# Clipped difference moved to ScalarE, a second load of x by rows, a gathered bias, and a grouped norm that runs behind, in a two-layer hybrid encoder

## The chip, the cores and the metric

One core of a Trainium2 chip runs the whole step. The metric is the device time of one execution in microseconds. Engines are named as in the profile: PE (TensorE), PEld (its weight loads), DVE (VectorE), ACT (ScalarE), POOL (GpSimd), SP (SyncE, which issues every DMA of this kernel).

## The reference

Two layers work on 1024 prompt tokens and 64 sample tokens, width 1024. Each layer normalises x, projects it to 5204 columns, runs three branches on them (RG-LRU, sparse attention with an indexer and top-k, Mamba-2 SSD), and adds the projected mix to x. Cut to what the change touches:

```python
h = x * rsqrt(mean(x * x, -1) + eps) * norm_w                  # first norm of a layer
# SSD, in chunks; cum is the cumulated dt * a of a head
decay = exp(where(tril, cum[l] - cum[s], -inf))
y = (decay * (C @ B.T) * dt) @ xs + exp(cum) * (C @ state) + D * xs
y = y * silu(z)
y_c = rmsnorm(y.reshape(..., 2, 512)) * ssd_norm               # grouped norm
# attention over the selected keys
logits = q @ k.T / 8 + rel_bias[bucket(pos_k - pos_q)]
```

## The kernel before

Tokens stand in nine tiles of 128 (the ninth has 64) and three chunks CH of 384, 384 and 320 columns. Activations lie with features on the partitions. A projection keeps fp32 precision with three matmuls a block: high and low parts of the weights (`whi`, `wlo`, made on ACT at L212 and on DVE or POOL at L213) times high and low parts of the activations (`sth`, `stl`); lines L235 to L237 are these matmuls.

The first layer's start: `load_x` issues x transposed in eight 128-row pieces for each chunk (L260), and the first norm's sums are made by `first_sums`: a Square of each piece on ACT (L268), additions on DVE (L270), then `token_sums`, three matmuls against ones (L290). `rsqrt` is twelve small DVE operations, and `spread` lays its result out over the columns with one matmul (L281). Then come `hf`, its high and low parts, and the first two projections, of the index keys and index queries.

`spread_bias` runs once, at the end of the first layer's index stage: it multiplies a bucket table of 32x384 with rel_bias (L162), copies the result into a buffer `g2` of the pool that projection outputs also use (L164), and writes it 128 times over to DRAM as `biasd` (L165). `near_bias` reads from it, with a stride of 383, each row's own window of 256 positions (L994), and adds a large number to one block (L996). It is called for each of the two key-value groups of a layer; its tile `nb` has one buffer.

Between the index stage and attention, the top-k bisection (`junk` on DVE at L596, `junka` on ACT at L602), the convolutions (`u`, `th`, `raw`), the gates, the queries and the SSD tiles run interleaved. The order in which steps are written out is the table PLAN: `s0` and `s1` advance the SSD generator of group 0 or 1 by one step. After each projection `pace` advances the top-k by one bit, at a lower priority. Within this, a scheduler orders the instructions of each engine by priority and by its own model of when things are due; the order is then fixed, and each engine runs it in sequence.

`ssd_inputs` prepares a tile: it loads the cumulated sums of eight heads to all partitions (`cumB`, L730, two buffers), transposes, scales, and forms the decay in three steps: for each head, subtract the row's own value and clip at zero (L760, DVE, eight instructions a tile), Exp (L763, ACT), times `cbm` (L764, DVE). `ssd` then does a tile's matmuls and adds, and multiplies with the gate into `yC` (L822). Squares and their sums go to `sqS` on ACT and POOL (L824 to L826). After every third tile the grouped norm follows at once: `token_sums`, `rsqrt`, `spread`, and four DVE products (L837) with four writes to DRAM. `yC` and `sqS` have one buffer each.

Of the kernel before, what the change touches and what calls it, by code (L numbers as in the profile page):

```python
# [10 lines left out]
F32 = mybir.dt.float32  # L11
# [49 lines left out]
def bucket_table():  # L61

    t = np.zeros((32, 384), np.float32)
    for m in range(384):
        rel = m - 255
        n = abs(rel)
        b = max(i for i in range(16) if BUCKET_FROM[i] <= n) + (16 if rel > 0 else 0)
        t[b, m] -= 1.0
        t[15, m] += 1.0
    return t  # L70
# [18 lines left out]
def body(ctx, tc, I, O):  # L89
# [39 lines left out]
    def s2_bank():  # L129
        return bank("s2", 2)  # L130
# [21 lines left out]


    biasd = drp.tile([8, 128, 384], F32, name="biasd")

    def spread_bias(p):
        tab = p.tile([32, 384], F32, name="tab")
        SP.dma_start(tab, I["bucket_table"])
        rb = p.tile([32, 8], F32, name="rb")
        SP.dma_start(rb, I["rel_bias"])  # L160
        bp = s2_bank()
        PE.matmul(bp[:8, :384], rb, tab, start=True, stop=True)  # L162
        bv = lay.tile([128, 384], F32, name="g2", bufs=G2)[:8]
        S.activation(bv, bp[:8, :384], AF.Copy)  # L164
        SP.dma_start(biasd, bv[:, None, :].to_broadcast([8, 128, 384]))  # L165
# [89 lines left out]

    def load_x(ci):
        a, b = CH[ci]
        for d in range(8):
            X[d, ci] = xpool.tile([128, b - a], F32, name=f"X{d}_{ci}")
            SP.dma_start(X[d, ci], I["x_t"][128 * d:128 * d + 128, a:b])  # L260

    def first_sums(ci):

        a, b = CH[ci]
        acc = xpool.tile([128, 384], F32, name="xacc", bufs=2)[:, :b - a]
        for d in range(8):
            sq = xpool.tile([128, 384], F32, name="xsq", bufs=4)[:, :b - a]
            S.activation(sq if d else acc, X[d, ci], AF.Square)  # L268
            if d:
                V.tensor_tensor(acc, acc, sq, op=OP.add)  # L270
        return token_sums(acc, ci)
# [13 lines left out]
    def token_sums(sqs, ci):  # L285

        ps = s2_bank()
        for t in range(3):
            n = rows_of(3 * ci + t)
            PE.matmul(ps[:n, t:t + 1], sqs[:, t * 128:t * 128 + n], ones[:, 0:1], start=True, stop=True)  # L290
        ss = small.tile([128, 3], F32, name="ssg")
        if ci == 2:
            V.memset(ss, 1.0)
            V.tensor_copy(ss[:, :2], ps[:, :2])
            V.tensor_copy(ss[:TS, 2:3], ps[:TS, 2:3])
        else:
            V.tensor_copy(ss, ps[:, :3])
        return ss

    for l in range(DEPTH):  # L300
# [31 lines left out]
        with ExitStack() as st:  # L332
# [11 lines left out]
            if l == 0:  # L344
                load_x(2)
                SP.dma_start(pk[1], I["par"][1])


            for ci, (a, b) in enumerate(CH):
                ss = token_sums(sqs[ci], ci) if l else first_sums(ci)  # L350
# [121 lines left out]
        with ExitStack() as st:  # L472
# [100 lines left out]
            if l == 0:  # L573
                spread_bias(p)
# [142 lines left out]
        def ssd_inputs(g, tt):  # L717
# [40 lines left out]

            for h in range(8):
                V.tensor_scalar(cumB[:n, h, :n], cumB[:n, h, :n], ctk[:n, tt, 8 * g + h:8 * g + h + 1], 0.0,  # L760
                                op0=OP.subtract, op1=OP.min)
            cB = cumB[:n, :, :n]
            S.activation(cB, cB, AF.Exp)  # L763
            V.tensor_tensor(cB, cB, cbm[:n, None, :n].to_broadcast([n, 8, n]), op=OP.mult)  # L764
            return xsc, C_, eB, bt, xdt, xde, cB

        def ssd(g):
# [4 lines left out]
            ready = ssd_inputs(g, 0)  # L772
            for k, tt in enumerate(order):
# [8 lines left out]
                if k % 3 == 0:  # L782
                    yC = p.tile([128, 4, 384], F32, name="yC", bufs=1)
                    sqs = p.tile([128, 384], F32, name="sqS", bufs=1)
# [41 lines left out]
                G.tensor_tensor(sqs[:, cc:cc + n], sq[:, 0, :n], sq[:, 1, :n], op=OP.add)  # L826
                yield
                if k % 3 < 2:
                    continue

                w = b0 - a0
                ss = token_sums(sqs, ci)
                r = rsqrt(ss, 3, 1.0 / 512, "g")
                rp = s2_bank()
                spread(r, 3 * ci, rp)
                for i in range(4):
                    V.scalar_tensor_tensor(yC[:, i, :w], yC[:, i, :w], par[:, 104 + 4 * g + i:105 + 4 * g + i], rp[:, :w],  # L837
                                           op0=OP.mult, op1=OP.mult)
                    SP.dma_start(ycd[4 * g + i][:, a0:b0], yC[:, i, :w])
                yield  # L840
# [150 lines left out]
        def near_bias(g):  # L991

            nb = kp.tile([128, 4, 256], F32, name="nb")
            SP.dma_start(nb, bass.AP(tensor=biasd.tensor, offset=biasd.offset + 4 * g * 128 * 384 + 127,  # L994
                                     ap=[[383, 128], [128 * 384, 4], [1, 256]]))
            V.tensor_scalar(nb[0:64, :, 192:256], nb[0:64, :, 192:256], BIG, None, op0=OP.add)  # L996
            return nb
# [193 lines left out]
def packed(x):  # L1191
# [3 lines left out]
    a = {"rel_bias": f("rel_bias"), "bucket_table": bucket_table()}  # L1195
    a["x_t"] = np.concatenate([f("x_prompt")[0], f("x_sample")[0]]).T
# [55 lines left out]
```

## Time and profile before

| | us |
|---|---|
| median of 3 runs | 2112.63 (2110.53 to 2113.01) |
| the profiled execution's own time | 2118.68 |
| its span in the trace | 2116.9 |
| busy: PE, DVE, ACT, POOL | 1975.6, 1614.3, 1132.9, 654.5 |

How to read the rows below. In a row of busy time by stretch the columns are: the stretch in us from the start; its length; busy us and (x instructions) of PE, PEld, DVE, ACT and POOL, or of one engine where the row is of one line alone; the granted TensorE clock as a share; the DMA engines' busy share; GB/s. A row of the timeline has the start, the duration, engine, line, operation, output<-inputs, sizes and count, and in brackets how long the engine stood before it and what ended that. A row of waits says who waited for whom: us in total, times, longest. In a row of a group the figures behind the bar are busy us and mean ns of one, then idle us before it. Instructions on one engine overlap by some 0.1 us, so eight in a row take less than eight means. A busy PE is not PE at its peak, since matmuls are pipelined.

### The profile page before, as it was taken

The numbers are of one execution on the slowest core, as the hardware profiler recorded it, in microseconds if no ns is written. First come the engines' busy times: TensorE is split into PE (matmuls) and PEld (weight loads), VectorE is DVE, ScalarE is ACT, GpSimd is POOL, SyncE is SP. The second block draws the span as 40 slices with busy tenths as digits, with TensorE's granted clock in tenths as the row PEclk, the third lists the DMA queues.
The fourth block names the chain that finished last, engine by engine and source line by source line (L and its number), as shares of the span: only waits on it lengthen the run. The fifth ranks groups of instructions, "written<-read, shape, count | busy, mean of one in ns | idle before, by whom it ended". The sixth has DMA issues, their size and how long they took to land.

```text
span 2116.9 us, 34794 instructions
## 1 busy us (share of the span) xinstructions
PE 1975.6 (93%) x12076; PEld 1767.8 (84%) x12076; DVE 1614.3 (76%) x4102; ACT 1132.9 (54%) x2244; POOL 654.5 (31%) x561
## 2 busy tenths in 40 slices
PE   5989989888999899999999999988899998999999
PEld 5889988878898788866998999887888897888589
DVE  8668999999886875475287889999998778556723
ACT  5558967622465454445255798664324565444521
POOL 3012243433332332142430222443334225223420
PEclk9999999999999999999999999999999998999999
DMA  4135353353533642332641343534454326334145
GB/s 137 55 64 155 95 143 119 101 172 104 139 90 101 208 143 90 107 100 88 199 143 55 94 116 101 161 106 127 118 153 119 118 104 207 108 91 131 57 132 171
DMA packets 253368, 255.11 MB, mean 121 GB/s; under 512 B 31048, under 2 KB 233192, under 8 KB 253192
## 3 DMA queue, kind: packets, MB, share of 16 engines
q1 hardware_dynamic: 253192, 252.89, 39.9%
q8 instruction: 95, 1.56, 0.3%
q14 instruction: 81, 0.66, 0.1%
HBM read 176.68 MB, written 76.14 MB: 119 GB/s over the span
## 4 chain that ended last, share of the span: by engine, by line
PE 51%; DVE 29%; DMA 9%; issue 5%; ACT 3%; SPq 1%; POOL 1%; DVEq 0%; ACTq 0%; POOLq 0%
PE mm L236 12%; PE mm L237 12%; PE mm L235 11%; PE s L1119 4%; PE tp L1114 3%; PE s L1089 3%; DVE junk L596 3%; DVE u L878 3%; DMA cumB<-cumd 3%; DVE cumB L760 3%; DMA biasd<-g 2%; PE s L534 1%; PE s L904 1%; ACT junka L602 1%; DVE cumB L764 1%
## 5 line engine op out<-in xcount | busy, mean ns | idle before, releaser
L213 POOL TENSOR_TENSOR wlo<-wraw,whi 128x1024 fp32r<-128x1024 f32 x80 | 198.1, 2476 | 390.8 <-ACT whi L212 378.1
L602 ACT ACTIVATE junka<-sc,cand 128x768 bf16<-128x768 f32 x248 | 239.1, 966 | 24.7 <-DVE cand L622 20.6
L212 ACT ACTIVATE whi<-wraw 128x1024 fp32r<-128x1024 f32 x130 | 137.1, 1054 | 148.1 <-PE mm L236 89.3
L1096 ACT ACTIVATE lg<-lg,mx 128x512 f32<-128x512 f32 (+8 forms) x144 | 111.3, 773 | 108.8 <-DVE mx L1092 108.0
L1081 POOL TENSOR_TENSOR nbm<-nb,shared 128x256 f32<-128x256 f32 (+1 forms) x112 | 81.3, 729 | 231.1 <-DVE mx L1092 208.9
L878 DVE SCALAR_TENSOR_TENSOR u<-raw,parh,u 128x384 f32<-128x384 f32 (+1 forms) x198 | 144.7, 736 | 1.9 <-ACT u L872 0.8
L1116 ACT ACTIVATE pT<-tp 128x512 f32<-128x512 f32 (+1 forms) x164 | 90.2, 568 | 101.8 <-PE tp L1114 99.9
L596 DVE TENSOR_SCALAR_CACHE_REDUCE junk<-sc,cand 128x384 bf16<-128x384 f32 (+4 forms) x194 | 140.1, 752 | 0.7
L1089 PE MATMUL s<-kst,qst 128*128 128x512 f32 (+4 forms) x448 | 120.6, 361 | 9.7 <-DVE mx L1092 9.3
L1114 PEld LDWEIGHTS tp<-identr,lg 128*128 128x128 f32 (+2 forms) x656 | 71.8, 140 | 46.9 <-issue 39.7
L1114 PE MATMUL tp<-identr,lg 128*128 128x128 f32 (+2 forms) x656 | 107.3, 278 | 0.7 <-DVE lg L1099 0.7
L1119 PE MATMUL s<-pT,vt 128*64 128x256 f32 (+2 forms) x656 | 103.9, 392 | 1.6 <-ACT pT L1116 1.6
L1099 DVE TENSOR_SCALAR lg<-lg,ri 128x512 f32<-128x512 f32 (+8 forms) x144 | 98.1, 681 | 3.5
L760 DVE TENSOR_SCALAR cumB<-cumB,ctk 128x128 f32<-128x128 f32 (+1 forms) x288 | 83.3, 353 | 22.1 <-DMA cumB<-cumd 19.7
L1164 DVE TENSOR_TENSOR xl<-xl,mm 128x384 f32<-128x384 f32 (+1 forms) x40 | 21.4, 540 | 92.9 <-PE mm L237 84.7
L1089 PEld LDWEIGHTS s<-kst,qst 128*128 128x128 f32 (+1 forms) x448 | 71.5, 187 | 24.0 <-DVE mx L1092 16.4
L1092 DVE CUSTOM_DVE_ANT_0 lg<-s,shared 128x512 f32<-128x512 f32 (+4 forms) x112 | 61.8, 552 | 38.4 <-PE s L1089 32.4
L235 PE MATMUL mm<-sth0a,whi 128*128 128x384 f32 (+1 forms) x228 | 81.5, 360 | 7.8 <-DVE sth0a L974 2.6
L213 DVE TENSOR_TENSOR wlo<-wraw,whi 128x1024 fp32r<-128x1024 f32 x50 | 63.5, 1269 | 26.4 <-ACT whi L212 25.9
L236 PE MATMUL mm<-stl0a,whi 128*128 128x384 f32 (+1 forms) x228 | 79.6, 349 | 2.8 <-POOL stl0a L977 2.5
L798 POOL TENSOR_TENSOR hT<-hT,dec 128x512 f32<-128x512 f32 x28 | 40.7, 1454 | 131.4 <-DMA ycd<-yC 57.7
L236 PE MATMUL mm<-stl7a,whi 128*128 128x384 f32 (+1 forms) x228 | 78.6, 345 | 2.2 <-DVE stl7a L977 2.2
(477 smaller groups left out, 6977.5 us busy)
## 6 DMA issues: line engine op xcount, KB each, us to landing
wraw<-in_w_in_dram SPq DMA_DIRECT2D x82, 512.0 KB, 3.7
wraw<-in_w_out_dram SPq DMA_DIRECT2D x48, 512.0 KB, 4.2
cumB<-cumd SPq DMA_DIRECT2D x32, 512.0 KB, 5.2
xsd<-u SPq DMA_DIRECT2D x48, 192.0 KB, 2.3
gz<-gzd SPq DMA_DIRECT2D x32, 256.0 KB, 3.9
xsc<-xsd SPq DMA_DIRECT2D x32, 256.0 KB, 3.5
eB<-cumd SPq DMA_DIRECT2D x56, 128.0 KB, 3.5
gzd<-g SPq DMA_DIRECT2D x32, 192.0 KB, 1.9
```

What stands on the lines that cost most here:

```text
L212: S.activation(hi, raw, AF.Copy)
L213: eng.tensor_tensor(lo, raw, hi.bitcast(F32), op=OP.subtract)
L235: PE.matmul(ps, hi[:, k, :], xh[ci][:, c0:], start=k == 0, stop=False)
L236: PE.matmul(ps, hi[:, k, :], xl[ci][:, c0:], start=False, stop=False)
L237: PE.matmul(ps, lo[:, k, :], xh[ci][:, c0:], start=False, stop=k == len(xs) - 1)
L596: V.tensor_scalar(junk, sc[j][:n], thr, None, op0=op, op1=OP.add, accum_out=out)
L602: S.activation(junk, sc[j][:n], AF.Sign, scale=-1.0, bias=cand, accum_out=out)
L760: V.tensor_scalar(cumB[:n, h, :n], cumB[:n, h, :n], ctk[:n, tt, 8 * g + h:8 * g + h + 1], 0.0, op0=OP.subtract, op1=OP.min)
L878: V.scalar_tensor_tensor(u, raw[:, j:j + n], w[:, wbase + j * wstride:wbase + j * wstride + 1], u, op0=OP.mult, op1=OP.add)
L1089: PE.matmul(ps[:nq, :b - a], qst[:, h, :nq], kst[:, g, pt, kbase + a:kbase + b], start=pt == 0, stop=pt == 1)
L1114: PE.transpose(ps[:n, i * nq:(i + 1) * nq], lgs[h][:nq, j * 128:j * 128 + n], ident[:nq, :nq])
L1119: PE.matmul(av[64 * b:64 * b + 64, :, :nq], vt[:n, vj, 64 * g:64 * g + 64], pT[:n, 2 * b:2 * b + 2, :nq], start=j == 0, stop=j == nb_ - 1)
```

## The change

Four edits. The bucket table, its matmul and the write of `biasd` go; the host hands over the near bias already gathered by position (an input of 2x128x4x256) and a row of far biases, and `near_bias` loads the first and forms far minus near on DVE, one instruction a head. Each chunk of x is also loaded by rows into `xr` (L246 in the changed kernel), ahead of the transposed pieces, and one Square with an accumulated sum on ACT gives the sums of 128 tokens; `first_sums` goes. The subtraction with its clip becomes a Relu on ACT with a scale of -1 and the row's value as bias, and the Exp takes a scale of -1. The grouped norm is cut into `sums` and `products`, of which one runs at the end of each following SSD tile; after the last tile what is left runs at once. `yC` and `sqS` get the pool's two buffers.

```diff
-    biasd = drp.tile([8, 128, 384], F32, name="biasd")
-    def spread_bias(p):
...
-        PE.matmul(bp[:8, :384], rb, tab, start=True, stop=True)
-        S.activation(bv, bp[:8, :384], AF.Copy)
-        SP.dma_start(biasd, bv[:, None, :].to_broadcast([8, 128, 384]))
...
     def load_x(ci):
         a, b = CH[ci]
+        for t in range(3):
+            n = rows_of(3 * ci + t)
+            xr = xpool.tile([128, DM], F32, name="xr", bufs=6)
+            SP.dma_start(xr[:n], I["x_r"][a + 128 * t:a + 128 * t + n])
+            S.activation(xr[:n], xr[:n], AF.Square, accum_out=ssx[ci][:n, t:t + 1])
         for d in range(8):
...
-                ss = token_sums(sqs[ci], ci) if l else first_sums(ci)
+                ss = token_sums(sqs[ci], ci) if l else ssx[ci]
...
             for h in range(8):
-                V.tensor_scalar(cumB[:n, h, :n], cumB[:n, h, :n], ctk[:n, tt, 8 * g + h:8 * g + h + 1], 0.0,
-                                op0=OP.subtract, op1=OP.min)
-            cB = cumB[:n, :, :n]
-            S.activation(cB, cB, AF.Exp)
+                S.activation(cB[:, h, :], cB[:, h, :], AF.Relu, scale=-1.0, bias=ctk[:n, tt, 8 * g + h:8 * g + h + 1])
+            S.activation(cB, cB, AF.Exp, scale=-1.0)
             V.tensor_tensor(cB, cB, cbm[:n, None, :n].to_broadcast([n, 8, n]), op=OP.mult)
...
+        def grouped_norm(g, ci, yC, sqs):
+            a, b = CH[ci]
+            r = []
+            def sums():
+                r.append(rsqrt(token_sums(sqs, ci), 3, 1.0 / 512, "g"))
+            def products():
+                rp = s2_bank()
+                spread(r[0], 3 * ci, rp)
+                for i in range(4):
+                    V.scalar_tensor_tensor(yC[:, i, :b - a], yC[:, i, :b - a], par[:, 104 + 4 * g + i:105 + 4 * g + i],
+                                           rp[:, :b - a], op0=OP.mult, op1=OP.mult)
+                    SP.dma_start(ycd[4 * g + i][:, a:b], yC[:, i, :b - a])
+                return True
+            return [sums, products]
...
-                    yC = p.tile([128, 4, 384], F32, name="yC", bufs=1)
-                    sqs = p.tile([128, 384], F32, name="sqS", bufs=1)
+                    yC = p.tile([128, 4, 384], F32, name="yC")
+                    sqs = p.tile([128, 384], F32, name="sqS")
...
+                if due and due.pop(0)():
+                    yield
                 yield
...
+                if k % 3 == 2:
+                    due += grouped_norm(g, ci, yC, sqs)
+            for part in due:
+                part()
+            yield
...
-            SP.dma_start(nb, bass.AP(tensor=biasd.tensor, offset=biasd.offset + 4 * g * 128 * 384 + 127,
-                                     ap=[[383, 128], [128 * 384, 4], [1, 256]]))
+            SP.dma_start(nb, I["near_bias"][g])
+            for h in range(4):
+                V.tensor_scalar(nb[:, h, :], nb[:, h, :], far_bias[:, 4 * g + h:4 * g + h + 1], -1.0,
+                                op0=OP.subtract, op1=OP.mult)
```

PE at the very start, before (`xacc` holds summed squares, `dg` the diagonal that `spread` multiplies with ones, `s` and `mm` are PSUM banks):

```order
L290 MATMUL s_263<-ones,xacc 128x1 x3
L290 MATMUL s_407<-ones,xacc 128x1 x3
L281 MATMUL s_269<-dg,ones 128x384
L290 MATMUL s_543<-ones,xacc 128x1 x2
L290 MATMUL s_543<-ones,xacc 64x1
L235 MATMUL mm<-sth0a,whi 128x384
L235 MATMUL mm<-sth0a,whi 128x128
```

The same place in the changed kernel:

```order
L260 MATMUL s_271<-dg,ones 128x384
L215 MATMUL mm<-sth0a,whi 128x384
L216 MATMUL mm<-stl0a,whi 128x384
L217 MATMUL mm<-sth0a,wlo 128x384
L215 MATMUL mm<-sth1a,whi 128x384
```

The sums of all three chunks stood ahead of the first projection matmul; now one spread does, and the two projections of the first chunk (384 and 128 columns wide) no longer alternate.

ACT at the tile of 64 rows and the one behind it in the first layer's SSD group 0, before:

```order
L862 ACTIVATE raw<-mm 128x256
L863 ACTIVATE raw<-mm 128x64
L872 ACTIVATE u<-raw,parh 128x323
L763 ACTIVATE cumB<-cumB 64x8x64
L859 ACTIVATE raw<-mm 128x384
L887 ACTIVATE th<-u 128x384
L746 ACTIVATE bt<-tp 64x128
```

ACT behind the same tile (`bt` 64x128 is its transpose) in the changed kernel:

```order
L724 ACTIVATE bt<-tp 64x128
L863 ACTIVATE u<-raw,parh 128x323
L878 ACTIVATE th<-u 128x384
L739 ACTIVATE cumB<-cumB,ctk 128x128 x8
L850 ACTIVATE raw<-mm 128x384
L580 ACTIVATE junka,cnt<-sc_641,cand 128x768
L580 ACTIVATE junka,cnt<-sc_642,cand 128x896
L740 ACTIVATE cumB<-cumB 128x1024
```

Eight Relus stand in ACT's queue ahead of a copy out of a PSUM bank (`raw`) and of the sign counts; the Exp follows some places behind them.

PE at the end of the first layer's SSD group 1, the last grouped norm, before:

```order
L235 MATMUL mm<-sth2a,whi 128x384
L290 MATMUL s_7468<-ones,sqS 128x1
L290 MATMUL s_7468<-ones,sqS 64x1
L236 MATMUL mm<-stl2a,whi 128x384
L237 MATMUL mm<-sth2a,wlo 128x384
```

The same place in the changed kernel:

```order
L215 MATMUL mm<-sth2a,whi 128x384
L216 MATMUL mm<-stl2a,whi 128x384
L269 MATMUL s_7399<-ones,sqS 128x1
L269 MATMUL s_7399<-ones,sqS 64x1
L217 MATMUL mm<-sth2a,wlo 128x384
```

The last sums stand one matmul further back, within the same projection block.

## Rows read from the trace of the kernel before

**Rows 1.** The page's first part, busy time by engine, and its chain by engine.
```profile
PE 1975.6 (93%) x12076; PEld 1767.8 (84%) x12076; DVE 1614.3 (76%) x4102; ACT 1132.9 (54%) x2244; POOL 654.5 (31%) x561
...
PE 51%; DVE 29%; DMA 9%; issue 5%; ACT 3%; SPq 1%; POOL 1%; DVEq 0%; ACTq 0%; POOLq 0%
```
**Rows 2.** Busy time by stretch, all engines.
```profile
170.00:250.00 80.00, 78.10 (x467) 77.52 (x466) 69.97 (x197) 73.96 (x153) 19.04 (x9) 1.00 0.44 129
250.00:550.00 300.00, 270.34 (x1682) 251.31 (x1680) 288.44 (x698) 153.66 (x309) 112.08 (x83) 0.96 0.44 127
...
1210.00:1290.00 80.00, 80.00 (x482) 79.93 (x481) 70.28 (x199) 75.30 (x157) 19.04 (x9) 1.00 0.46 134
1290.00:1590.00 300.00, 267.65 (x1692) 247.50 (x1691) 289.19 (x702) 153.38 (x307) 114.04 (x83) 0.98 0.43 127
```
**Rows 3.** Busy time by stretch of line L760 alone, on DVE.
```profile
250.00:550.00 300.00, 32.38 (x96) 0.96 0.44 127
550.00:710.00 160.00, 6.50 (x32) 0.99 0.37 114
...
1290.00:1590.00 300.00, 30.91 (x97) 0.98 0.43 127
```
**Rows 4.** Waits over the whole span, around cumB.
```profile
ACT cumB L763 <- DVE cumB L760: 79.1, 26, 5.2
...
DVE cumB L760 <- DMA cumB<-cumd: 19.7, 13, 3.2
```
**Rows 5.** Busy time of the same work in the first and in the second layer.
```profile
108.00:245.00 137.00, 129.38 (x761) 125.09 (x761) 106.38 (x304) 105.03 (x218) 26.00 (x15) 0.98 0.43 110
1159.30:1284.70 125.40, 125.25 (x758) 122.66 (x758) 106.20 (x304) 104.69 (x217) 25.38 (x15) 1.00 0.36 107
```
**Rows 6.** The chain in order of time, and ACT's timeline, at the bias write.
```profile
120.61 33.54 DMA biasd<-g
...
154.23 0.38 ACT L679 ACTIVATE g<-tp 128x256 f32<-128x256 f32 x1 [9.32 <-DMA biasd<-g]
```
**Rows 7.** Busy time by stretch at the start; the last column is GB/s.
```profile
5.00:10.00 5.00, 0.00 (x0) 0.00 (x0) 3.68 (x11) 3.33 (x9) 0.00 (x0) 1.00 0.98 333
10.00:15.00 5.00, 1.44 (x6) 1.35 (x6) 4.40 (x20) 4.20 (x8) 0.00 (x0) 1.00 1.03 375
```
**Rows 8.** Timeline: the first two weight splits; projection matmuls, first, second chunk's, last.
```profile
10.62 1.06 ACT L212 ACTIVATE whi<-wraw 128x1024 fp32r<-128x1024 f32 x1 [1.07 <-DMA wraw<-in_w_in_dram]
...
16.59 1.06 ACT L212 ACTIVATE whi<-wraw 128x1024 fp32r<-128x1024 f32 x1 [1.06 <-DMA wraw<-in_w_in_dram]
...
27.06 0.79 PE L235 MATMUL mm<-sth0a,whi 128*128 128x384 f32 x2 [0.31 <-ACT sth0a L365]
...
38.54 0.39 PE L235 MATMUL mm<-sth0a,whi 128*128 128x384 f32 x1
...
55.95 0.31 PE L237 MATMUL mm<-sth7b,wlo 128*128 128x320 f32 x1
```
**Rows 9.** Near bias: durations of L996 (min/median/max ns), a 128x256 form, POOL's wait.
```profile
L996 DVE TENSOR_SCALAR nb<-nb x4: 277/281/287, 718.6 to 1891.3; 64x256 f32<-64x256 f32 x4
...
L1099 DVE TENSOR_SCALAR lg<-lg,ri 128x256 f32<-128x256 f32 x4 | 1.9, 479 | 0.1
...
POOL nbm L1081 <- DVE nb L996: 12.6, 4, 5.5
```
**Rows 10.** ACT groups by form: two operands per partition, none, and 128 columns.
```profile
L872 ACT ACTIVATE u<-raw,parh 128x384 f32<-128x384 f32 x48 | 33.7, 702 | 11.8 <-DMA xsd<-u 8.0 <-DVE junk L653 3.3
L859 ACT ACTIVATE raw<-mm 128x384 f32<-128x384 f32 x64 | 30.6, 478 | 20.7 <-PE mm L237 20.4
...
L746 ACT ACTIVATE bt<-tp 128x128 f32<-128x128 f32 x32 | 8.6, 270 | 33.0 <-DVE cbm L744 33.0
```
**Rows 11.** PE's wait for the grouped norm's sums, and the later of its places.
```profile
PE s L290 <- POOL sqS L826: 13.5, 2, 7.0
...
1738.31 0.48 PE L290 MATMUL s<-ones,sqS 128*128 128x1 f32 x4
```

More of the change, by code (lines that the diff above doesn't have):

```diff
@@ L58, with buckets @@
 P_DT, P_A, P_D, P_QK, P_ALL = 160, 176, 192, 200, 328
[L61 to L70, printed above, removed]
+def buckets():
+    rel = np.arange(256)[None, :] - np.arange(128)[:, None] - 128
+    return np.searchsorted(BUCKET_FROM, np.abs(rel), side="right") - 1 + 16 * (rel > 0)
 def rows_of(t):
@@ L151, in body @@
         G.memset(kb[:, j:j + 1], float(2 * kk[j] - nks[j] - 1))
-    biasd = drp.tile([8, 128, 384], F32, name="biasd")
-    def spread_bias(p):
[L157 to L161, printed above, removed]
-        PE.matmul(bp[:8, :384], rb, tab, start=True, stop=True)
-        bv = lay.tile([128, 384], F32, name="g2", bufs=G2)[:8]
-        S.activation(bv, bp[:8, :384], AF.Copy)
-        SP.dma_start(biasd, bv[:, None, :].to_broadcast([8, 128, 384]))
     def rsqrt(ss, n, scale, tag, rows=128):
@@ L254, in body @@
     pk = [lay.tile([128, P_ALL], F32, name=f"pk{l}") for l in range(DEPTH)]
+    far_bias = const.tile([128, 8], F32, name="far_bias")
+    ssx = [small.tile([128, 3], F32, name=f"ssx{ci}", bufs=1) for ci in range(3)]
+    V.memset(ssx[2], 1.0)
     def load_x(ci):
         a, b = CH[ci]
+        for t in range(3):
[3 more added lines that the diff above has]
+            S.activation(xr[:n], xr[:n], AF.Square, accum_out=ssx[ci][:n, t:t + 1])
         for d in range(8):
@@ L260, in load_x @@
             SP.dma_start(X[d, ci], I["x_t"][128 * d:128 * d + 128, a:b])
[L262 to L271, printed above, removed]
     def spread(r, t0, dst):
@@ L346, in body @@
                 SP.dma_start(pk[1], I["par"][1])
+                SP.dma_start(far_bias, I["far_bias"])
             for ci, (a, b) in enumerate(CH):
-                ss = token_sums(sqs[ci], ci) if l else first_sums(ci)
+                ss = token_sums(sqs[ci], ci) if l else ssx[ci]
                 rp = s1_bank()
@@ L572, in body @@
             SP.dma_start(cumd, cumt)
-            if l == 0:
-                spread_bias(p)
         steps(zs)
@@ L757, in ssd_inputs @@
                             op=OP.mult)
+            cB = cumB[:n, :, :n]
             for h in range(8):
-                V.tensor_scalar(cumB[:n, h, :n], cumB[:n, h, :n], ctk[:n, tt, 8 * g + h:8 * g + h + 1], 0.0,
-                                op0=OP.subtract, op1=OP.min)
-            cB = cumB[:n, :, :n]
-            S.activation(cB, cB, AF.Exp)
+                S.activation(cB[:, h, :], cB[:, h, :], AF.Relu, scale=-1.0, bias=ctk[:n, tt, 8 * g + h:8 * g + h + 1])
+            S.activation(cB, cB, AF.Exp, scale=-1.0)
             V.tensor_tensor(cB, cB, cbm[:n, None, :n].to_broadcast([n, 8, n]), op=OP.mult)
             return xsc, C_, eB, bt, xdt, xde, cB
+        def grouped_norm(g, ci, yC, sqs):
[12 more added lines that the diff above has]
+            return [sums, products]
         def ssd(g):
@@ L772, in ssd @@
             ready = ssd_inputs(g, 0)
+            due = []
             for k, tt in enumerate(order):
@@ L826, in ssd @@
                 G.tensor_tensor(sqs[:, cc:cc + n], sq[:, 0, :n], sq[:, 1, :n], op=OP.add)
+                if due and due.pop(0)():
+                    yield
                 yield
[L828 to L840, printed above, removed]
+                if k % 3 == 2:
[3 more added lines that the diff above has]
+            yield
         PCH = ((0, 384), (384, 768), (768, PW))
@@ L1194, in packed @@
     tiles = lambda a: a.reshape(DEPTH, -1, 128)
-    a = {"rel_bias": f("rel_bias"), "bucket_table": bucket_table()}
-    a["x_t"] = np.concatenate([f("x_prompt")[0], f("x_sample")[0]]).T
+    b = f("rel_bias")
+    a = {"near_bias": b[buckets()].transpose(2, 0, 1).reshape(2, 4, 128, 256).transpose(0, 2, 1, 3),
+         "far_bias": np.repeat(b[15:16], 128, 0)}
+    a["x_r"] = np.concatenate([f("x_prompt")[0], f("x_sample")[0]])
+    a["x_t"] = a["x_r"].T
     w = f("w_in").reshape(DEPTH, 8, 128, EIN)
```

## The prediction

> **What bounds the kernel now.** I read the engines' busy time and the chain of waits first [rows 1]. TensorE is busy for 1975.6 of 2116.9 us, which looks like the bound, but only 51% of the chain runs through it; VectorE holds 29%. So the bound changes by stage, and the busy time by stretch comes next [rows 2]. Each layer has two kinds of stretch. In 170 to 250 us and 1210 to 1290 us (convolutions and top-k, no SSD tiles) TensorE is busy 78.1 and 80.0 of 80 us. In 250 to 550 us and 1290 to 1590 us (the same loops with the SSD tiles among them) VectorE is busy 288.4 and 289.2 of 300 us, TensorE 270.3 and 267.7, ScalarE 153.7 and 153.4. There VectorE is the bound, at 96%, and TensorE has gaps. The eight subtractions with a clip per tile at L760 are the part of that load which the change takes away: 32.4 and 30.9 us in those two stretches, 6.5 us in 550 to 710 [rows 3]. Their order matters too: VectorE stands 19.7 us there for the transfer of cumB, and ScalarE stands 79.1 us for VectorE before the exponential [rows 4].
>
> Two other places are bound by something else. The stretch from the last index scores to the first SSD tile does the same work in both layers (304 VectorE instructions each), but takes 137.0 us in the first and 125.4 in the second [rows 5]. What only the first has is the write of the bias table: it is on the chain for 33.54 us, and ScalarE stands 9.32 us because the write still reads a buffer that its next output needs [rows 6]. And at the start the transfers run at 333 to 375 GB/s [rows 7], while the first projection matmul comes at 27.06 us [rows 8].
>
> **The change, part by part.**
>
> Bias table gone. The 33.54 us write leaves, with one matmul, one ScalarE copy and three issues on the SP queue. If the first layer then runs as the second does, that is 137.0 - 125.4 = 11.6 us [rows 5]; the least is 0, if the weights behind it on the queue come late anyway. The 9.32 us wait has no other cause [rows 6], so I take -11.
>
> The near bias is loaded ready and corrected: four more VectorE operations of 128x256 at each of four loads. The nearest rows are 281 ns (64 rows, same line) and 479 ns (a 128x256 TENSOR_SCALAR), so 16 x 0.28 to 0.48 = 4.5 to 7.7 us [rows 9]. The load itself stays 512 KB. GpSimd waits for this tile at all four places [rows 9], so nothing covers all of it, but GpSimd is not the bound there: 0 to +8, I take +3.
>
> The start. Sums come from a second load of x by rows: 4.46 MB more on the queue (8 x 512 KB and 256 KB). At 340 GB/s the first 1.57 MB costs 4.6 us, all of it 13. In return 21 VectorE additions, nine matmuls and the order change: before, TensorE does all three chunks' sums ahead of the first projection matmul, now only the first chunk's spread stands there. The first weights' split, at 10.62 us, moves to about 15.2 and ends at 16.3; the first matmul follows at about 17, not 27. It does not all count: the second block's weights are behind x of the second chunk, so their split moves from 16.59 to about 16.6 + 9.2 = 25.8, and its low part ends near 28. From there 2.7 us of narrow matmuls for the first chunk and the second and third chunks, 38.54 to 56.26 before [rows 8], are left: 28 + 2.7 + 17.7 = 48.5 against 56.3. Ends: -11 (the whole earlier start), +13 (every byte late and nothing gained). I take -7.
>
> The clipped difference on ScalarE. Off VectorE go 63.3 us in the two bound stretches. If VectorE stayed the bound, all of it would leave the time; if the queue behind cumB's transfer bound them, none. Between: TensorE gets 482 matmuls through 80 full us [rows 2], so the 1682 and 1692 of the bound stretches need about 279 and 281 us: at most 21 and 19 us can go at that rate. That limit is rough, since the SSD's matmuls are narrower. I take half of VectorE's share, -32, with ends -63 and 0. In 550 to 710 us no engine is alone; 6.5 us goes from VectorE there, I count -1 a layer, so -2.
>
> ScalarE pays for it. An operand per partition costs it (702 - 478) / 2 = 112 ns each, from two 128x384 forms with two and none; a 128x128 copy takes 270 ns, so one Relu is about 380 ns, some 0.3 us in a row [rows 10]: 288 of them 84 us. In the bound stretches it has 146 us of 300 free. In 170 to 250 it has 6 of 80 free, TensorE 2: 16 Relus, 4.8 us a layer, land there ahead of evacuations that TensorE's banks need. 0 to +10 for both layers; I take +6. The wait for cumB moves from VectorE's queue to ScalarE's: behind it stand convolution copies and sign counts, and then VectorE and TensorE. VectorE's 19.7 us [rows 4] bounds that at either engine; it is within the ends above.
>
> The Trainium skill speaks against this move: "ScalarE: Activation LUTs", section "Rules for kernel authors", puts relu, max, min and add on VectorE and not on ScalarE, as VectorE does more elements in a cycle. By that rule the move costs 84 - 63 = 21 us instead of giving 32. The rows for the bound stretches (VectorE 96%, ScalarE 51%) say that here it is the fuller engine that counts.
>
> The grouped norm a tile and two behind. Same instructions. TensorE's wait for its sums is 13.5 us, but in two places alone; one is at 1738.31 us, the end of the second layer's last group, and the other is its like in the first layer [rows 11]. There the new code runs sums and products right after the last tile as before, so this wait stays. The earlier groups show next to none. The four writes of each chunk pass later through SP; who reads them comes at the layer's end. A second buffer of yC frees the next tile: -6 to +6, I take -1.
>
> **Sum.** -11 + 3 - 7 - 32 - 2 + 6 - 1 = -44. The profiled execution took 2118.68 us (span 2116.9), 6 above the median of the runs, 2112.63; the difference applies to either. Predicted: 2112.63 - 44 = 2068.6.
>
> **Rivals.** *VectorE's whole share counts* (-63 rather than -32, ScalarE's +6 gone): -81, 2032 us. For it: 96% busy with next to no waits but cumB's. Against: TensorE's rate gives only 40. *The SSD stage does not shorten*, since the path from cumB's transfer through Relu, exponential and product replaces the one through VectorE: -11 + 3 - 7 = -15, 2098 us. For it: VectorE waits for that transfer now [rows 4], and no buffer is added for it. Against: 300 us hold 96 subtractions [rows 3], twelve tiles, so some 25 us for each. *ScalarE becomes the bound* (slower than before): it takes 84 us of Relus and 20 us of waiting, with PSUM evacuations behind in order. It decides once more than about 15 of these 104 us reach TensorE while the SSD stage gives nothing; with a third, 2112.6 - 15 + 35 = 2133 us. For it: 92 to 94% busy in 170 to 250. Against: the bound stretches have room for it. The Trainium skill's rule above would be this case. *The change does not speed the start*: x twice keeps TensorE waiting as long as before; that is +7 on any case, 2076 on mine.
>
> **How the numbers follow.** My forecast, with the start's rival and a spread of 20 either side, 0.60; whole share 0.14; no shorter stage 0.16; ScalarE bound 0.08; everything cancelling to within 4 us 0.02. The range for 8 in 10 runs from 2034 to 2100: it holds the forecast, most of the no-gain case and half of the whole-share case. About 0.2% (4 us) is what a measurement of this kernel can tell from no change. Faster 0.89, same 0.03, slower 0.08.
>
> **What would show it.** Right: no 9 us ScalarE wait near 145 us and 125 us for the stretch of [rows 5]; first projection matmul near 17 us and the three chunks done near 48; VectorE's share in the SSD stretches under 95% with TensorE's busy share up, each stretch 10 to 21 us shorter; ScalarE busy about 80 us longer. Wrong: ScalarE standing for cumB's transfer as long as the stretch gained, TensorE waiting for bank evacuations in 170 to 250 us, or a second transfer of x that delays the second chunk past 40 us.

## The result, and the profile of the changed kernel

The changed kernel takes 2087.18 us (median of 4 runs, 2084.96 to 2090.63) against 2112.82 us for the kernel before in the same session: a ratio of 0.9881, 95% interval 0.9864 to 0.9898, or -25.6 us. The forecast was -44 with a range of -78 to -12. The time lies in the range and the sign is right, but 18 us of the forecast gain are missing, and they go with one of the four edits, the grouped norm.

The page's busy time by engine and its chain by engine, of the changed kernel, answer to [rows 1]:

```profile
PE 1964.9 (94%) x12056; PEld 1753.2 (84%) x12056; DVE 1542.9 (74%) x3805; ACT 1209.1 (58%) x2525; POOL 652.9 (31%) x561
...
PE 53%; DVE 24%; DMA 9%; ACT 7%; issue 5%; SPq 1%; POOL 1%; DVEq 0%; ACTq 0%; POOLq 0%
```

VectorE has lost 71 us of busy time, and ScalarE has gained 76 (about 80 forecast). Busy time by stretch, with the columns of [rows 2]:

```profile
170.00:250.00 80.00, 78.67 (x477) 77.89 (x476) 71.60 (x194) 76.49 (x162) 17.34 (x7) 1.00 0.32 105
250.00:550.00 300.00, 278.86 (x1760) 255.43 (x1759) 276.36 (x619) 186.79 (x423) 125.03 (x97) 0.98 0.48 136
...
1290.00:1590.00 300.00, 276.45 (x1742) 253.44 (x1742) 275.89 (x609) 185.26 (x414) 122.36 (x96) 0.97 0.46 134
```

In the two stretches that VectorE bound it is now busy 92% of the time instead of 96%, and TensorE is busy 8.5 to 8.8 us more. In 170 to 250 us ScalarE rises to 76.5 of 80 us, and TensorE does not fall.

The start, in the timeline of TensorE: the first projection matmul and the last one of the third chunk, which answer to [rows 8]; and the transfer rate from 5 to 10 us (last column), which answers to [rows 7]:

```profile
15.53 0.69 PE L215 MATMUL mm<-sth0a,whi 128*128 128x384 f32 x1 [2.16 <-ACT sth0a L345]
...
48.65 0.31 PE L217 MATMUL mm<-sth7b,wlo 128*128 128x320 f32 x1
```
```profile
5.00:10.00 5.00, 0.00 (x0) 0.00 (x0) 1.15 (x7) 3.30 (x6) 0.00 (x0) 1.00 1.05 390
```

The first matmul comes at 15.5 us (27.06 before, 17 forecast), and the last matmul of the third chunk starts at 48.65 (55.95 before; the three chunks were forecast to be done near 48). The work of [rows 5], from the last index scores to the first SSD tile, now takes this stretch:

```profile
100.70:228.50 127.80, 126.28 (x769) 122.90 (x768) 105.30 (x285) 107.15 (x231) 25.59 (x16) 1.00 0.36 108
```

It is 127.8 us long instead of 137.0, and the write of the bias table and the wait of 9.32 us behind it [rows 6] are gone with it.

What is new is a group of waits. From the list of waits over the whole span (who waited for whom: us in total, times, longest):

```profile
PE s L260 <- DVE dg L258: 29.8, 8, 11.7
...
PE tp L1013 <- ACT pT L1008: 10.7, 5, 4.8
...
PE mm L215 <- DVE sth0a L965: 9.4, 4, 3.8
...
ACT cumB L739 <- DMA cumB<-cumd: 59.9, 23, 7.6
...
POOL nbm L1074 <- DVE nb L989: 20.5, 4, 8.6
```

TensorE no longer waits for the grouped norm's sums (13.5 us in [rows 11]). It waits for `dg`, the diagonal that `spread` multiplies (9.5 us before), and where attention begins for `pT` (4.4 before; it is the copy of a key tile there) and for `sth0a` (2.6 before). Of the 29.8 us for `dg`, 11.7 are TensorE's first wait of the program, which comes with the new start; the other 18.1 are new waits. The chain in order of time has a piece at the end of the first layer's SSD part that the chain of before did not have among its longest:

```profile
689.24 8.38 DMA lg<-in_cache_att_k_dram
```

`lg` there is the tile into which attention's cached keys are loaded. It belongs to none of the four edits.

### The profile page after: what moved, and what is told of

It is laid out like the page before. It is cut to its first block, busy times and chain, and to the rows that moved or that the text cites. A ratio compares the mean times of both kernels' runs of the same rounds, so it can differ in the third digit from the quotient of the medians.

```text
span 2088.8 us, 34723 instructions
## 1 busy us (share of the span) xinstructions
PE 1964.9 (94%) x12056; PEld 1753.2 (84%) x12056; DVE 1542.9 (74%) x3805; ACT 1209.1 (58%) x2525; POOL 652.9 (31%) x561
## 3 DMA queue, kind: packets, MB, share of 16 engines
q1 hardware_dynamic: 251904, 255.73, 40.2%
## 4 chain that ended last, share of the span: by engine, by line
PE 53%; DVE 24%; DMA 9%; ACT 7%; issue 5%; SPq 1%; POOL 1%; DVEq 0%; ACTq 0%; POOLq 0%
PE mm L216 12%; PE mm L215 12%; PE mm L217 12%; PE s L1112 4%; PE tp L1107 4%; PE s L1082 3%; ACT junka L580 3%; DVE junk L574 3%; DVE u L869 2%; DMA cumB<-cumd 2%; PE s L895 1%; PE s L514 1%; DMA eB<-cumd 1%; ACT cumB L739 1%; DVE cumB L741 1%
## 5 line engine op out<-in xcount | busy, mean ns | idle before, releaser
L869 DVE SCALAR_TENSOR_TENSOR u<-raw,parh,u 128x384 f32<-128x384 f32 (+1 forms) x198 | 138.5, 707 | 7.1 <-ACT u L863 4.5
L739 ACT ACTIVATE cumB<-cumB,ctk 128x128 f32<-128x128 f32 (+1 forms) x288 | 88.6, 384 | 64.5 <-DMA cumB<-cumd 59.9
L1092 DVE TENSOR_SCALAR lg<-lg,ri 128x512 f32<-128x512 f32 (+8 forms) x144 | 90.2, 629 | 2.9
L734 POOL TENSOR_TENSOR xsc<-xsc,pk 128x512 f32<-128x512 f32 (+1 forms) x36 | 46.4, 1288 | 135.5 <-PE tp L728 122.0
L1082 PEld LDWEIGHTS s<-kst,qst 128*128 128x128 f32 (+1 forms) x448 | 70.0, 183 | 20.5 <-DVE mx L1085 11.5
L193 DVE TENSOR_TENSOR wlo<-wraw,whi 128x1024 fp32r<-128x1024 f32 x50 | 62.5, 1250 | 31.6 <-ACT whi L192 31.5
L821 POOL TENSOR_TENSOR sq<-sq 128x256 f32<-128x256 f32 (+1 forms) x36 | 34.9, 969 | 159.6 <-ACT sq L820 159.6
```

Source lines behind the costliest of these rows:

```text
L193: eng.tensor_tensor(lo, raw, hi.bitcast(F32), op=OP.subtract)
L869: V.scalar_tensor_tensor(u, raw[:, j:j + n], w[:, wbase + j * wstride:wbase + j * wstride + 1], u, op0=OP.mult, op1=OP.add)
L1082: PE.matmul(ps[:nq, :b - a], qst[:, h, :nq], kst[:, g, pt, kbase + a:kbase + b], start=pt == 0, stop=pt == 1)
```

## The experiments

Each kernel was timed in five rounds beside the kernel before. The table gives the ratio with its 95% interval, and the difference in us on the median of before (2115 us in all three sessions).

| kernel | ratio | interval | us |
|---|---|---|---|
| bias edit alone | 0.9966 | 0.9951 to 0.9981 | -7.2 |
| start edit alone | 0.9966 | 0.9953 to 0.9979 | -7.2 |
| clip on ScalarE alone | 0.9849 | 0.9823 to 0.9875 | -31.9 |
| delayed norm alone | 1.0047 | 1.0031 to 1.0063 | +9.9 |
| changed kernel without the delayed norm | 0.9791 | 0.9771 to 0.9811 | -44.2 |
| before with an unused 7680 bytes | 1.0031 | 1.0018 to 1.0044 | +6.6 |
| delayed norm, gate tile in the keys' pool | 1.0053 | 1.0033 to 1.0072 | +11.2 |
| changed kernel, gate tile in the keys' pool | 0.9851 | 0.9832 to 0.9871 | -31.5 |
| delayed norm, gate tile in the outer pool | 0.9998 | 0.9987 to 1.0010 | -0.4 |
| changed kernel, gate tile in the outer pool | 0.9802 | 0.9787 to 0.9817 | -41.9 |
| before without the clip | 0.9892 | 0.9874 to 0.9909 | -22.8 |
| without delayed norm, three buffers of cumB | 0.9819 | 0.9802 to 0.9837 | -38.3 |

### One edit at a time

Each of four kernels is the kernel before with one part of the diff: the hunks of `biasd`, `spread_bias` and `near_bias`; those of `load_x`, `first_sums` and `ss`; those of the clip; and those of `grouped_norm`, `due` and the two buffers.

> The kernel before with the bias edit alone: no bucket table, no write of 128 copies to DRAM, the near bias loaded by position and corrected with four more VectorE operations. Theory 1 (the sum of the prediction): -11 for the write and the wait behind it, +3 for the corrections: -8, 2105 us. Reading of the changed kernel's trace: the lead over before grows from 7.3 to 16.5 us between 123 and 170 us and is lost by nothing there, so -9 at 250 us and what the corrections cost in attention behind it. Rival (the weights behind the write come late anyway): 0 at 250 us, +3 in all.

> The kernel before with the second load of x by rows alone, and the sums from it. Theory 1: -7, 2106 us, first projection matmul near 15 us instead of 27, the three chunks done 7 us sooner. Rival (the lead at the start is given back where the conv stage waits for something else): at most -2.

> The kernel before with the clip moved to ScalarE alone (Relu with the row's value as bias, Exp with a scale of -1). Theory 1 (half of VectorE's share, ScalarE pays 6): -28, 2085 us. Reading of the changed kernel's trace (the lead grows by about 12 us from 250 to 710 us in the first layer, 6 in the second, and part of it is lost in attention): -8 to -14, 2099 to 2105 us. Rival (SSD stage not shortened): 0 to +6.

> The kernel before with the grouped norm a tile and two behind, alone, and two buffers of yC and sqS. Theory 1: -1, within 6 us of before either way. Rival (the norm is what shortened the SSD stage in the changed kernel, not the clip): -8 to -12, 2101 to 2105 us. Rival (moved writes and products cost): +4 or more.

The bias edit gives -7.2 where the prediction's sum has -8, the start edit -7.2 where it has -7, and the clip -31.9 where it has -28 (-32 and -2, with +6 for ScalarE). My reading of the changed kernel's own trace (-8 to -14 for the clip) was the worse of the two theories: that trace mixes the clip's gain with a loss from another edit. The delayed norm, to which the prediction gave -1, costs 9.9 us alone. It is neither neutral nor the source of the gain, and its cost lies beyond what I had put as its upper end (+6). The number fits the rival "moved writes and products cost", but by the runs below it goes when a tile of attention is moved.

What the clip does shows when the same stretch of work is cut out of each trace: from the 16th to the 34th of the 130 splits of weights (`whi` on ScalarE) in the first layer, and from the 79th to the 97th in the second. Before, clip alone, changed kernel without the delayed norm, changed kernel (columns as in [rows 2]):

```profile
244.47:560.64 316.17, 286.08 (x1774) 266.14 (x1773) 304.16 (x742) 163.79 (x329) 117.52 (x87) 0.96 0.44 126
1262.65:1563.59 300.94, 270.94 (x1690) 253.12 (x1690) 290.07 (x703) 168.98 (x344) 111.30 (x78) 0.98 0.42 123
```
```profile
243.44:541.51 298.07, 280.52 (x1785) 263.24 (x1784) 275.86 (x644) 195.14 (x440) 112.93 (x87) 0.98 0.46 135
1242.58:1527.32 284.74, 269.34 (x1706) 255.14 (x1705) 270.00 (x631) 197.20 (x443) 107.77 (x79) 0.98 0.45 132
```
```profile
230.41:530.73 300.32, 282.57 (x1785) 265.04 (x1784) 276.71 (x644) 195.21 (x440) 113.64 (x87) 0.96 0.47 134
1234.21:1520.99 286.78, 267.95 (x1706) 253.23 (x1705) 270.65 (x631) 196.96 (x442) 110.96 (x79) 0.98 0.43 131
```
```profile
227.12:536.17 309.05, 288.16 (x1824) 265.92 (x1823) 288.88 (x666) 200.23 (x455) 125.12 (x96) 0.98 0.47 135
1235.84:1535.78 299.94, 276.39 (x1723) 258.15 (x1722) 281.03 (x639) 199.11 (x445) 115.10 (x83) 0.97 0.44 131
```

The clip alone shortens these stretches from 316.2 to 298.1 us and from 300.9 to 284.7, 18 and 16 us: the "10 to 21 us shorter" of the prediction. VectorE's busy time falls by 28 and 20 us, and TensorE's gaps from 30.1 to 17.6 us and from 30.0 to 15.4. With the bias and the start edit beside it nothing changes (300.3 and 286.8). With the delayed norm the stretches are 309.1 and 299.9 long. Part of that is not a loss: TensorE does 1824 matmuls in the first of them instead of 1785, and 1723 instead of 1706 in the second, since SSD tiles come a step earlier.

### What the clip's place is worth

In this kernel the eight subtractions are left out and nothing stands for them:

```diff
-            for h in range(8):
-                V.tensor_scalar(cumB[:n, h, :n], cumB[:n, h, :n], ctk[:n, tt, 8 * g + h:8 * g + h + 1], 0.0,
-                                op0=OP.subtract, op1=OP.min)
```

> The kernel before with the subtraction and its clip left out altogether (the decay is then the exponential of the cumulated sum alone): VectorE has its relief and ScalarE pays nothing. Theory 1 (relief worth half of VectorE's share and ScalarE pays 6): -34 to -40, some 6 us beyond the clip on ScalarE alone (-32). Rival (VectorE's whole share counts and ScalarE takes half of it back): -55 to -65. Rival (ScalarE's 85 us of Relus are free): -30 to -33.

It gives -22.8 us, less than moving the clip to ScalarE (-31.9; the intervals, 0.9823 to 0.9875 and 0.9874 to 0.9909, just touch). No theory said this. Two things follow. No cost of ScalarE's 88.6 us of Relus shows in this pair; their price is not isolated by it, since the order of the instructions differs too. And the relief of VectorE is not a fixed number. The page's first part of the kernel with the clip on ScalarE and of the one without it:

```profile
PE 1969.2 (94%) x12076; PEld 1762.6 (85%) x12076; DVE 1533.3 (74%) x3814; ACT 1209.7 (58%) x2532; POOL 643.9 (31%) x561
```
```profile
PE 1977.0 (94%) x12076; PEld 1773.1 (85%) x12076; DVE 1562.2 (75%) x3814; ACT 1133.3 (54%) x2244; POOL 654.5 (31%) x561
```

VectorE runs the same 3814 instructions in both, and is busy 28.9 us longer in the second: 62 comparisons of 128x7 values (`keep<-cnt,lim`) take 246 ns each in the first and 353 in the second, on average, for one. The section on the hardware below shows how one and the same instruction can take 0.17 or 2.37 us. That this makes the 9 us between the two kernels was not isolated.

### Where the delayed norm loses

Every load is issued on SP. Four pieces of its timeline at the end of the first layer's SSD part (start, duration, and what is loaded): the kernel before, the changed kernel, the kernel before with a tile of 7680 unused bytes, and the changed kernel with the gate tile in the outer pool. `ycd<-yC` is the four writes of the last grouped norm, `lg` the keys of attention.

```profile
698.63 0.74 SPq L1006 DMA_DIRECT2D lg<-kvd  x1
699.43 0.74 SPq L1007 DMA_DIRECT2D lg<-in_cache_att_k_dram  x1
...
709.79 2.12 SPq L839 DMA_DIRECT2D ycd<-yC  x4
```
```profile
682.03 1.79 SPq L758 DMA_DIRECT2D ycd<-yC  x4
...
687.95 1.25 SPq L999 DMA_DIRECT2D lg<-kvd  x1
689.24 2.94 SPq L1000 DMA_DIRECT2D lg<-in_cache_att_k_dram  x1
```
```profile
710.49 1.79 SPq L840 DMA_DIRECT2D ycd<-yC  x4
716.63 0.59 SPq L1007 DMA_DIRECT2D lg<-kvd  x1
717.26 2.44 SPq L1008 DMA_DIRECT2D lg<-in_cache_att_k_dram  x1
```
```profile
674.63 0.81 SPq L999 DMA_DIRECT2D lg<-kvd  x1
675.50 0.73 SPq L1000 DMA_DIRECT2D lg<-in_cache_att_k_dram  x1
686.10 1.81 SPq L758 DMA_DIRECT2D ycd<-yC  x4
```

Before, the keys are loaded 11 us ahead of the last norm's writes. In the changed kernel they come 6 us behind them, and the key transposes that open attention wait for them: before its first copy of a key tile (`pT`) ScalarE stands 8.69 us for the keys, against 3.08 before. The edit that moved them is the second buffer of `yC` and `sqS`. It makes the SSD's pool 7680 bytes longer in every partition. In the built program the pool ended at byte 103,520, and attention's pool, allocated from the other end, begins at 110,304. With the second buffers the SSD's pool ends at 111,200 (111,328 in the changed kernel, where the far biases and the start's sums lie below it). The two now share about 1 KB, and attention's first tiles are the keys. The third piece above shows it in a kernel with no instruction added or left out; the edit is one unused tile:

```diff
         sa = pool(stC, L("SA"), bufs=2)
+        sa.tile([128, 1920], F32, name="pad", bufs=1)
```

> The kernel before with one unused tile of 7680 bytes a partition at the head of the SSD's pool: not one instruction more or less, but the pool now reaches to byte 111,200 as it does in the kernel with the delayed norm, where attention's pool begins at byte 110,304. Theory 2 (the norm's second buffers cost because attention's key tiles now share bytes with the SSD's pool, so that their loads wait for the last norm's writes): key loads after the four writes at the end of each layer instead of 10 us ahead of them, first key transposes some 10 to 20 us later, +6 to +14 us in all. Rival (what costs is the norm's new order): 0.

It costs 6.6 us, the low end of the theory's range. Up to the first attention tile its trace runs level with before (the 43rd split of weights at 712.8 us against 713.0). The first copy of keys comes 21 us later (724.5 against 703.2), and the first softmax weights of attention (the `pT` of L1116 before) 7 us later.

The reverse test takes the overlap away and keeps the delayed norm. Attention's pool is made 1 KB shorter, by giving the gate's tile a place in another pool:

```diff
-            ga = p.tile([128, 2, 128], F32, name="ga", bufs=1)
+            ga = kp.tile([128, 2, 128], F32, name="ga")
```

> The kernel before with the delayed norm, and one 1 KB tile of attention (the gate's, ga) moved to the pool of the keys, so that attention's pool begins at byte 111,328, behind the end of the SSD's. Theory 2: the key loads stand ahead of the last norm's writes again and the 10 us that the delayed norm costs alone are gone: -4 to +2 against before. Rival (the norm's new order costs): +8 to +12 as without the move.

> The changed kernel with the same tile moved, nothing else. Theory 2: 15 to 22 us faster than the changed kernel, 2065 to 2072 us at a median of before of 2113, about level with the kernel that leaves the delayed norm out. Rival (the norm's new order costs): within 4 us of the changed kernel.

By the times the theory would have fallen: the delayed norm alone gives +11.2, where its rival said, and the changed kernel gains 6 us, short of 15 to 22. The trace says otherwise: the keys are loaded early again and attention starts 11 us sooner in the first layer, but the gain is lost at the end of each layer to a new wait, the matmul behind the last residual additions. From the list of waits of that kernel:

```profile
PE mm L235 <- DVE xl L1178: 13.4, 2, 6.7
```

Without the move it is 2.0 us. The gate's tile is read until attention's last write. The tiles of the last residual, `xl`, lie where the keys' pool was, though not on the gate tile's own bytes (58,208 to 64,352 against 95,072 to 96,096 in the first layer of the built program); even so their first load starts 0.5 us after the last gate write has landed (986.13 and 985.66 us; 2034.45 and 2034.01 in the second layer), where without the move it starts 8 us ahead of it. So by these times they wait for the whole keys' pool, which the gate tile keeps open longer. The first move made the same kind of wait in another place. The pool that lives through the output projection (`sqp`) stays open past that point:

```diff
-            ga = p.tile([128, 2, 128], F32, name="ga", bufs=1)
+            ga = sqp.tile([128, 2, 128], F32, name="ga")
```

> The kernel before with the delayed norm, and the gate tile of attention (ga, 1 KB) moved to the pool that lives through the output projection, not to the keys' pool. Theory 2, mended (in the first move the keys' pool closed late, so that the last residual loads waited 6.7 us at the end of a layer): key loads ahead of the last norm's writes and no wait at the layer's end; about 7 us a layer back against the first move, -4 to +2 against before. Rival (the new order itself costs): +6 or more.

> The changed kernel with the same move. Theory 2, mended: 10 to 16 us faster than the changed kernel, -38 to -44 against before, 2071 to 2077 us. From the traces the delayed norm still loses 6 to 10 us a layer in the SSD stage beside the other edits and gets 5 back where attention begins, so 0 to 6 us behind the kernel without it. Rival (nothing of the cost is room): within 4 us of the changed kernel.

Now the delayed norm alone is level with before (0.9998, against 1.0047 without the move), and the changed kernel goes from 0.9881 to 0.9802, some 17 us. Both came out as expected. TensorE's waits at the beginning of attention, the delayed norm alone and then with the gate tile in the outer pool:

```profile
PE tp L1034 <- ACT pT L1029: 10.7, 5, 4.9
PE mm L235 <- DVE sth0a L988: 8.1, 2, 4.3
```
```profile
PE tp L1034 <- ACT pT L1029: 5.2, 2, 3.9
...
PE mm L235 <- DVE sth0a L988: 1.9, 4, 0.9
```

The kernel that leaves the delayed norm out was run as the opposite end:

> The changed kernel with the grouped norm as it was before (bias, start and clip edits only). Theory 1 (the three edits add up, and the delayed norm is the only loss): -7 -8 -32 = -47 against before, 2066 us on the median of before in this call; 18 to 25 us faster than the changed kernel. Rival (the gains of the three edits overlap, and the norm costs no more than the 10 us it costs alone): about -36, 2078 us.

It gives -44.2, close to the sum of the three edits alone (-46.3) and 19 us better than the changed kernel. Against the changed kernel with the gate tile moved the intervals overlap (0.9771 to 0.9811 and 0.9787 to 0.9817). So the delayed norm together with that move is worth nothing that can be measured here.

The level times hide two things that differ. This table cuts one execution of each of three kernels (their runs spread by some 5 us), first and second layer, in us: the SSD part runs from the 16th (79th) split of weights to the last norm's writes, the start of attention from there to the first softmax weights.

| | SSD part | start of attention |
|---|---|---|
| changed kernel without the delayed norm | 453.4, 471.7 | 32.8, 32.0 |
| changed kernel | 454.9, 480.8 | 38.8, 40.2 |
| changed kernel, gate tile in the outer pool | 457.4, 478.5 | 28.9, 29.0 |

The changed kernel loses 6 and 8 us at the start of attention, where its keys come late. Beside that its SSD parts are some 11 us longer in all, and the move does not give this back; it makes the start of attention shorter than in the kernel that never had an overlap, by 7 us in all. What goes with the longer SSD parts is TensorE's wait for `dg`, here without the delayed norm and then with it and the gate tile moved; in both some 12 us are the program's first wait:

```profile
PE s L260 <- DVE dg L258: 14.0, 3, 12.0
```
```profile
PE s L260 <- DVE dg L258: 31.8, 8, 11.8
```

That this wait is what makes the SSD parts longer was not isolated. Nor was the gate tile moved in a kernel without the delayed norm, so what the move gives by itself is not known.

What the key loads wait for when the pools overlap is not the tile whose bytes they take. In the built program that is `hS`, a state that TensorE last reads at 585.8 us in the changed kernel, 102 us ahead of the first key load. That load starts 2.6 us after the last norm's writes have landed (687.95 and 685.31 us; 1722.48 and 1719.87 in the second layer). So by these times, as with `xl`, the wait is for the whole earlier pool.

### The wait for cumB

```diff
-            cumB = p.tile([128, 8, 128], F32, name="cumB")
+            cumB = p.tile([128, 8, 128], F32, name="cumB", bufs=3)
```

> The kernel with the bias, start and clip edits (no delayed norm) and a third buffer of cumB, which ends at byte 107,744 and so stays clear of attention's pool. Theory 1 (the wait for cumB's transfer now stands on ScalarE, 53 us in all, and little of it reaches TensorE): -8 to 0 against the same kernel with two buffers. Rival (the wait is what keeps the SSD stage from shortening more): -10 to -20.

ScalarE's wait for the transfer, with two buffers and with three:

```profile
ACT cumB L739 <- DMA cumB<-cumd: 52.6, 27, 8.1
```
```profile
ACT cumB L739 <- DMA cumB<-cumd: 19.9, 17, 2.8
```

33 us of waiting go, and the kernel is not faster: 0.9819, against 0.9791 with two buffers, with intervals that overlap. The wait is large and off the path. The rival in which the SSD stage would shorten further falls; theory 1 had -8 to 0 and got +6, so it missed as well, on the other side.

## Why the prediction was right, and which step was not

*Start*: -7 forecast, -7.2 alone. The steps hold one by one: first matmul at 17 forecast and 15.5 measured, three chunks done near 48 forecast and at 49.0 measured. The sign of being wrong, a second chunk delayed past 40 us, did not come: that chunk begins at 30.4 us.

*Bias table and corrections*: -11 + 3 forecast, -7.2 alone. The stretch of [rows 5] fell by 9.2 instead of 11. The sixteen corrections take 348 ns each, 5.6 us, within the 4.5 to 7.7 that the prediction had, and GpSimd's wait for them [rows 9] went from 12.6 to 20.5 us:

```profile
L987 DVE TENSOR_SCALAR nb<-nb,far_bias x16: 345/348/354, 692.0 to 1865.5; 128x256 f32<-128x256 f32 x16
```

*Clip on ScalarE*: -32 - 2 + 6 = -28 forecast, -31.9 alone. The term in the bound stretches, half of VectorE's 63 us, was right in size (18 and 16 us). The +6 for ScalarE finds no support, though the time alone does not rule it out (the interval is -26 to -37). One Relu takes 388 ns in the changed kernel (380 forecast), and with the clip alone ScalarE is indeed busy 75.4 of 80 us in 170 to 250 us, but TensorE is busy 77.8 us there against 78.1 before, and the kernel with the Relus is not slower than the one without the clip:

```profile
L739 ACT ACTIVATE cumB<-cumB,ctk x288: 332/388/406, 161.8 to 1632.1; 128x128 f32<-128x128 f32 x128, 64x64 f32<-64x64 f32 x16
```
```profile
170.00:250.00 80.00, 77.81 (x464) 76.83 (x463) 67.53 (x176) 75.39 (x162) 18.96 (x9) 1.00 0.45 133
```

Three rivals fall with this: the whole of VectorE's share (-63), the stage that does not shorten, and ScalarE as the bound. The Trainium skill's rule that speaks against this edit ("ScalarE: Activation LUTs", section "Rules for kernel authors": relu, max, min and add on VectorE) would have left the clip where it was; here the measurement decides for ScalarE, by 31.9 us, in stretches where VectorE was 96% busy and ScalarE 51%.

*Grouped norm*: this is the step that failed. The prediction said "A second buffer of yC frees the next tile: -6 to +6, I take -1." Alone it costs 9.9 us, in the changed kernel 19 (0.9881 against 0.9791). 10 and 17 us come back when the gate tile is moved out of the way. In the changed kernel 14 us are lost at the start of attention, where the keys come late; the SSD parts, some 11 us longer beside the other edits, are a second loss that the prediction did not have, and its cause stays open. I had followed the moved instructions through every queue and had not asked whose bytes the new buffers lie in. The larger part of the cost falls on attention, which the edit does not touch, and no row of the trace of before shows it. What could have shown it was the order of the changed kernel on SP: the key loads stand behind the last norm's writes there and ahead of them before. The orders set beside each other ahead of the prediction are of PE and ACT, not of SP where attention begins.

A reading was wrong as well. The prediction put TensorE's two waits for the sums at the ends of the layers; the second row of [rows 11] was only one of the norm's places, and it shows no wait. The two waits of the kernel before stand at 394 us (6.5 us) and 1433 us (7.0 us), at first groups. The delayed norm did remove them. But the clip on ScalarE alone removes them too: neither that kernel nor the changed kernel without the delayed norm has such a wait.

The three sound edits make -46.3 alone and -44.2 together; the forecast was -44 in all, and the norm's 19 lead to the measured -25. All four do not add up: alone they make -36.4, so the norm costs 9 us more beside the others than by itself. The range, which reached to the case of a stage that does not shorten, held the time for a reason that it did not contain; that was luck.

**The better version.** Both kernels are beaten by two others: the changed kernel with the norm left as it was (0.9791, 2072.8 us) and the changed kernel with the gate tile in the outer pool (0.9802, 2071.9 us).

## What to carry to other kernels

A second buffer costs bytes, and bytes have neighbours: before giving a tile another buffer, look up which later pool begins where the longer pool would end, and whether its first loads stand early in their queue; here they waited for the whole earlier pool, not for the tile that they shared bytes with. When an engine at 96% sits beside one at 51%, moving work between them can pay even where the second takes longer for it, and here half of what the clip took on VectorE in the bound stretches came back. Time each edit of a bundle alone: one loss of 10 to 19 us hid behind three gains.

## What the runs showed of the hardware that was not expected

A VectorE instruction can take many times its own length when a long GpSimd instruction begins beside it. From the timeline of the kernel with the clip alone, VectorE and then GpSimd, and from the list of a line's instructions (min/median/max ns) of the kernel without the clip, the same instruction of 128x4 values:

```profile
403.54 2.37 DVE L634 TENSOR_SCALAR half<-M 128x4 int32<-128x4 int32 x1
```
```profile
403.17 2.72 POOL L213 TENSOR_TENSOR wlo<-wraw,whi 128x1024 fp32r<-128x1024 f32 x1
```
```profile
L634 DVE TENSOR_SCALAR half<-M x2: 170/170/171, 389.8 to 1420.3; 128x4 int32<-128x4 int32 x2
```

It takes 0.17 us by itself and 2.37 us when it starts 0.37 us into GpSimd's split of weights, and it ends as that ends (405.91 and 405.89 us). The Trainium skill ("SBUF — State Buffer", section "Who interferes with whom") says that a VectorE instruction in a two-port mode and GpSimd share a pair of ports as an exclusive lock, and that the later one blocks for the whole of the other's instruction. The two ends agree with that; which mode the instruction ran in no run here shows. GpSimd runs 80 such splits of about 2.4 us, and which VectorE instructions stand beside them depends on the order. In the kernel before, the eight subtractions of a tile take 1.66 us where nothing long runs beside them, and the longest single one of them 4.42 us (it starts at 1420.47 us, and GpSimd has three instructions end to end from 1420.43 to 1424.81):

```profile
287.38 1.66 DVE L760 TENSOR_SCALAR cumB<-cumB,ctk 128x128 f32<-128x128 f32 x8
```
```profile
L760 DVE TENSOR_SCALAR cumB<-cumB,ctk x288: 236/276/4418, 178.4 to 1665.8; 128x128 f32<-128x128 f32 x128, 64x64 f32<-64x64 f32 x16
```

At 1.66 us a tile the 36 tiles would take some 60 us, an estimate. So part of the 83 us that the clip took on VectorE was its neighbours' time and not its own, and a busy time read from a trace is not what an engine gets back when the work is removed: moved to ScalarE, those 83 us lower VectorE's busy time by 81 (1614.3 to 1533.3), and left out altogether by 52 (to 1562.2).
